# A fused two-block transformer kernel: all weight splits outside the top-k on VectorE, and every moving operand at one place within a KiB

## The chip, the core and the metric

The kernel runs on one core of one Trainium2 chip, as one launch. The metric is the device time of an execution in microseconds (us). The engines are named as in the profile: PE is TensorE's matmul, PEld its weight load, DVE is VectorE, ACT ScalarE, POOL GpSimd, SP SyncE, which issues most DMAs.

## What is computed

256 tokens of width 1024 go through a first block (windowed attention, a bidirectional RG-LRU, cross-attention to a memory, a gated merge, then a PEER layer of 16,384 experts) and through two hybrid layers (retention, a causal convolution of 31 taps, spatial gating, sliding-window attention, a gated merge, a gated FFN). All of it is float32. Cut to what matters here:

```python
h = rmsnorm(x, g_mix); proj = h @ w_in; ...          # first block
x = x + merged @ w_out
x = x + peer_ffn(rmsnorm(x, g_ffn), w_peer_q, sub_keys, u_tab, v_tab)
for l in range(2):                                    # hybrid layers
    z = rms_norm(x, norm1_g[l]) @ w_in[l]
    u = lax.conv_general_dilated(a * sigmoid(gate), conv_w, ...)   # 31 taps, per channel
    mix = jnp.sum(gates * branches, axis=2)
    x = x + mix @ w_out[l]
    gt, up = jnp.split(rms_norm(x, norm2_g[l]) @ w_ffn_in[l], 2, axis=-1)
    x = x + (silu(gt) * up) @ w_ffn_out[l]
```

The PEER layer is computed densely: `peer_u` and `peer_v` are multiplied whole, and the gates, which a top-k chooses, are spread over all experts by one-hot products.

## The kernel before

**Weights.** All weight matrices are cut into 128x128 blocks, and the host packs the 5416 blocks in the order of use. `Stream` (L41) brings them in: `_slot` (L69) takes eight blocks, a slot, and there are 677 slots. For a slot, SP loads the float32 values (`raw`, two slots in one 1 MB DMA, two buffers), ACT copies them rounded to float32r (`whi`, L88), and a subtraction leaves the rest (`wlo = raw - whi`, L91). This subtraction runs on DVE or on POOL: `pool_share = (m, d)` gives POOL the slots with `n * m % d < m`. In the program before it is (1, 2), every second slot, through the first block; (1, 1), every slot, from the second projection of the top-k; (0, 1), none, while the experts are computed; and (1, 2) again for both hybrid layers. `whi` and `wlo` have three buffers each, so the split runs up to three slots ahead of PE.

**Matmuls.** A product of two float32 matrices is three matmuls in float32r (`mm3`, L169): high by high, low by high, high by low. The weight block is the stationary operand, an activation row of 128 x 256 the moving one. One slot is 24 such matmuls.

**Activations.** `hh` and `hl` (L379, L380) hold the normed input's high and low part for every projection; `ga` holds the experts' activations. Other moving operands come from tiles of each stage's pool: `T8`, `T6`, `T4` of the first block (L415 to L422), `T4` of a layer (L1065), `fh`, `fl` and `raw` of the FFN. In the built program, `hh`, `hl` and `ga` start 704 bytes behind a multiple of 1024 bytes in a partition; the `T4` tiles of the layers at 352; the first block's tiles at ten places between 192 and 864; `fh` and `fl` at 192; the last three experts' `tail` at 64.

**Order.** The program is written as coroutines (`add`, `tick`): every second block taken from the stream gives waiting tasks a step, so convolution, attention and top-k are interleaved with the projections. A scheduling layer then sets the order on each engine, and each engine works through its list in that order. The slots' work has a high priority. The convolution of a layer is 124 instructions on DVE (L1121, "taps"), two for each step of its task and each issued after the latest subtraction on DVE (`tc.issue_after(ws.on_vector)`, L1120). DVE also does the low half of each activation split (L185, L188), the softmax sums and most evacuations; POOL adds up the gated merge (L621), a few products (L558, L1269, L1363) and some splits of a norm (L185).

Of the kernel before, what the change touches and what calls it, by code (L numbers as in the profile page):

```python
# [7 lines left out]
F32 = mybir.dt.float32  # L8
# [11 lines left out]
P = 128  # L20
S = 256
KD = 8
# [2 lines left out]
PRIO = 3000  # L25
RAW_BUFS = 2
SLOT_BUFS = 3
N_HA = 96
HALF = 64
TK_PACE = 20  # L30
# [22 lines left out]
class Stream:  # L53
# [3 lines left out]
    def __init__(self, K, pool, w):  # L57
        self.K, self.pool, self.w = K, pool, w
        self.order = []
        self.ticked = 0  # L60
        self.raw = None
        self.cur = None
        self.pool_share = (1, 2)

    def _dram(self, i):
        return self.w[i].rearrange("p (b c) -> p b c", c=P)
# [7 lines left out]
    def _slot(self):  # L74
        K, nc = self.K, self.K.nc
        n = len(self.order) // 8
        with K.tc.high_priority(offset=PRIO):
# [7 lines left out]
            src = self.raw[:, (n % 2) * 8:(n % 2) * 8 + 8, :]  # L85
            hi = self.pool.tile([P, 8, P], F32R, tag="whi", name="whi", bufs=SLOT_BUFS)
            lo = self.pool.tile([P, 8, P], F32R, tag="wlo", name="wlo", bufs=SLOT_BUFS)
            self.on_scalar = nc.scalar.activation(out=hi, in_=src, func=AF.Copy).ins  # L88
# [39 lines left out]
class Core:  # L128
# [111 lines left out]
    def transpose(self, out, in_):  # L240
        self.nc.tensor.transpose(out, in_, self.ident)

    def scr(self, name):
        return self.tp.tile([P, S], F32, tag="scr", name=name, bufs=N_SCR)

# [164 lines left out]
    def block1(self):  # L410
        tc, nc, a, ws = self.tc, self.nc, self.a, self.ws
        with ExitStack() as st:
            p = st.enter_context(tc.tile_pool(name="b1", bufs=1))

            def T8(dt=F32R):  # L415
                return p.tile([P, KD, S], dt, tag="t8", name="t8", bufs=2)

            def T6(dt=F32, w=S):
                return p.tile([P, 6, w], dt, tag="t6", name="t6", bufs=8)

            def T4(dt=F32):
                return p.tile([P, 4, S], dt, tag="t4", name="t4", bufs=5)  # L422

            def raw16():
                b = blocks(T6(F32R), T6(F32R), T6(F32R))
# [13 lines left out]
            t_rel = self.add(self.rel_bias(p), REL_AT)  # L439


            xl = T6(w=S + 3)
            nc.gpsimd.memset(xl[:, :, 0:2], 0.0)
            nc.gpsimd.memset(xl[:, :, S + 2:S + 3], 0.0)

# [288 lines left out]
    def peer(self):  # L734
# [4 lines left out]
        tc, nc, a, ws = self.tc, self.nc, self.a, self.ws  # L739
        with ExitStack() as st:  # L740
            p = st.enter_context(tc.tile_pool(name="pe", bufs=1))
# [5 lines left out]
            ga = [p.tile([P, 2, S], F32R, tag=f"ga{i}", name="ga") for i in range(2)]  # L747
            ha = p.tile([P, N_HA, S], F32, tag="ha", name="ha")
            hb = None

            def h(b):
                return ha[:, b, :] if b < N_HA else hb[:, b - N_HA, :]

# [17 lines left out]
            with tc.tile_pool(name="peg", bufs=1) as gp:  # L771
                hb = gp.tile([P, NBLK - N_HA, S], F32, tag="hb", name="hb")
                ws.pool_share = (0, 1)
# [5 lines left out]
                def build(c0, done):  # L779
# [19 lines left out]
                    def products(i, e2, m):  # L799
                        for o in range(0, T_OH, 4):  # L800
                            pg = self.bg.tile([P, 4, 2, HALF], F32, tag="bg", name="pgb")
                            for t in range(4):
# [9 lines left out]
                                                    op=ALU.add)  # L812
                            for b, t, c1, c2 in ((ha, 0, 0, N_HA), (hb, N_HA, N_HA, NBLK)):
                                k0, k1 = max(c1, c0), min(c2, c0 + w)
# [25 lines left out]

                cut = NBLK - N_HA
                for b0 in range(early, HALF, 4):
                    for b, k0, k1 in ((ha, b0, min(b0 + 4, HALF, cut)), (hb, max(b0, cut), min(b0 + 4, HALF))):
                        if k0 < k1:
                            o = HALF if b is ha else HALF - N_HA
                            nc.vector.tensor_tensor(out=ha[:, k0:k1, :], in0=ha[:, k0:k1, :],
# [29 lines left out]
                        u_block(ahead, h(ahead - done))  # L876
                        ahead += 1
                assert ahead == NBLK
                ws.pool_share = (1, 2)
                tl = self.tp.tile([P, LAST, 2, S], F32R, tag="ld", name="tail", bufs=1)  # L880
                tail = [weighted(NBLK - LAST + i, tl[:, i]) for i in range(LAST)]
            with tc.tile_pool(name="per", bufs=1) as gp:
# [40 lines left out]
    def topk(self, tp, i1, i2, gt, iot):  # L923
        nc, a, ws = self.nc, self.a, self.ws
# [85 lines left out]
        qts = {0: self.ld}  # L1010

        def picks():
            with self.tc.issue_after(ws.on_pool):
                nc.gpsimd.tensor_copy(io, self.cst[:, None, C_IO:C_IO + 16].to_broadcast([P, 32, 16]))
            for hq in range(4):
                for t in range(2):
                    while hq not in qts:
                        yield 1
                    unit(hq, t, qts[hq])
                    if hq == t == 1:  # L1020
                        with self.tc.issue_after(ws.on_pool):
                            nc.gpsimd.tensor_copy(iot, self.cst[:, C_IO:C_IO + P, None].to_broadcast([P, P, 2]))
                    yield TK_PACE
                    if hq == 3:
                        gates(t)
                        yield 2
                        turn(t)
            yield 4
# [25 lines left out]
    def mixers(self, l):  # L1054
        tc, nc, a, ws = self.tc, self.nc, self.a, self.ws
        with ExitStack() as st:
            p = st.enter_context(tc.tile_pool(name=f"m{l}", bufs=1))
            par = p.tile([P, P2_COLS], F32, tag="par2", name="par2")
            nc.scalar.dma_start(out=par, in_=a["par2"][l])
# [3 lines left out]
                return par[:, o:o + n]  # L1063

            def T4(dt=F32):  # L1065
                return p.tile([P, 4, S], dt, tag="t4", name="t4", bufs=13)

            def tmp(shape, tag, bufs=2, dt=F32):
                return p.tile(shape, dt, tag=tag, name=tag, bufs=bufs)
# [365 lines left out]
    def ffn(self, l):  # L1435
        tc, nc, a, ws = self.tc, self.nc, self.a, self.ws
        with ExitStack() as st:
            p = st.enter_context(tc.tile_pool(name=f"f{l}", bufs=1))
            fh = p.tile([P, FF, S], F32R, tag="fh", name="fh")
            fl = p.tile([P, FF, S], F32R, tag="fl", name="fl")  # L1440

# [167 lines left out]
```

## Time and profile before

| | |
|---|---|
| median of 3 runs | 2208.46 us (2206.96 to 2214.88) |
| the profiled execution | 2205.13 us |
| its span, first to last instruction | 2203.3 us |
| granted clock of PE, mean | 0.971 |
| PE busy | 2067.6 us (94%), 16818 matmuls |
| DVE busy | 1741.0 us (79%) |
| ACT busy | 1159.6 us (53%) |
| POOL busy | 734.2 us (33%) |

Stages in the profiled execution, by the first use of their slots: the first block to 350 us, the top-k to 500, the experts to 1189, layer 0's mixers to 1537 and its FFN to 1700, layer 1's mixers to 2042 and its FFN to the end. In each layer the first 155 to 165 us of the mixers hold the attentions, the retention and over half of the convolution; after them come the gated merge and the output projection. A busy PE is not a PE at its peak: every matmul is shown with about 280 ns, and matmuls that overlap follow each other at 113 ns or more, so a gap of less than some 170 ns does not show as idle time.

### The profile page before, as it was taken

To read this page: it belongs to the slowest core of one execution; us is meant where nothing else is said; L and a number is where in the kernel's file an instruction comes from. 1 tells how busy PE (TensorE), PEld (TensorE's weight loads), DVE (VectorE), ACT (ScalarE), POOL (GpSimd) and SP (SyncE) were. 2 spreads that over 40 slices of the span, in tenths; PEclk is the share of its full clock that TensorE was granted. 3 is DMA by queue.
4 is the path that set the end of the run, shared out by engine and by line. 5 is a ranking of instruction groups with operands and counts; after the bars stand their busy time and mean duration, and the time that the engine had idled before them with its cause. 6 is when DMAs were issued, how large, how long until landed. Compare 5 with 4: busy or idle time off the path is not lost. (4 is left out here: it accounts for less than half of the span.)

```text
span 2203.3 us, 41676 instructions
## 1 busy us (share of the span) xinstructions
PE 2067.6 (94%) x16818; PEld 2002.5 (91%) x16818; DVE 1741.0 (79%) x3117; ACT 1159.6 (53%) x1906; POOL 734.2 (33%) x361
## 2 busy tenths in 40 slices
PE   8879999959998999999998899999999889999999
PEld 7868999959998999999998778999999778999997
DVE  8837668998999888975557999976764999976772
ACT  5648654435554555545445555466555545465543
POOL 4424746830000000000003434654444434654443
PEclk9989999979999999999999999999999999999999
DMA  5343555424553444455554533454555533445554
GB/s 194 122 126 118 189 183 181 172 84 167 179 181 138 173 173 173 173 177 194 197 188 145 190 125 143 173 183 176 197 192 193 191 131 135 168 177 175 192 192 159
DMA packets 56925, 370.03 MB, mean 168 GB/s; under 512 B 6491, under 2 KB 10140, under 8 KB 13468
## 3 DMA queue, kind: packets, MB, share of 16 engines
q1 hardware_dynamic: 50256, 357.06, 45.5%
q10 hardware_dynamic: 6476, 10.31, 1.8%
q8 instruction: 131, 2.15, 0.4%
q14 instruction: 62, 0.51, 0.1%
HBM read 364.73 MB, written 2.62 MB: 167 GB/s over the span
## 5 line engine op out<-in xcount | busy, mean ns | idle before, releaser
L88 ACT ACTIVATE whi<-raw 128x1024 fp32r<-128x1024 f32 x677 | 716.5, 1060 | 731.0 <-PE acc L172 165.9
L91 POOL TENSOR_TENSOR wlo<-raw,whi 128x1024 fp32r<-128x1024 f32 x247 | 617.5, 2501 | 1324.6 <-ACT whi L88 1238.6
L91 DVE TENSOR_TENSOR wlo<-raw,whi 128x1024 fp32r<-128x1024 f32 x430 | 545.2, 1268 | 211.7 <-ACT whi L88 209.9
L171 PE MATMUL pu<-hh,whi 128*128 128x256 f32 x1024 | 291.0, 284 | 21.9 <-ACT whi L88 21.9
L173 PE MATMUL mm<-hh,wlo 128*128 128x256 f32 x1008 | 285.7, 284 | 7.3 <-DVE wlo L91 5.0
L173 PE MATMUL pu<-hh,wlo 128*128 128x256 f32 x1024 | 286.5, 280 | 0.0
L172 PE MATMUL pu<-hl,whi 128*128 128x256 f32 x1024 | 286.4, 280 | 0.0
L172 PE MATMUL mm<-hl,whi 128*128 128x256 f32 x1008 | 285.2, 283 | 0.0
L171 PE MATMUL mm<-hh,whi 128*128 128x256 f32 x1008 | 284.7, 282 | 0.0
L172 PE MATMUL acc<-ga,whi 128*128 128x256 f32 x1000 | 269.8, 279 | 5.1 <-DVE ga L185 5.1
L173 PE MATMUL acc<-ga,wlo 128*128 128x256 f32 x1000 | 269.2, 279 | 0.0
L171 PE MATMUL acc<-ga,whi 128*128 128x256 f32 x1000 | 249.3, 281 | 4.9 <-ACT ga L184 4.9
L1121 DVE SCALAR_TENSOR_TENSOR t<-up,hw,t 128x256 f32<-128x256 f32 x240 | 215.3, 901 | 3.7
L171 PEld LDWEIGHTS pu<-hh,whi 128*128 128x128 f32 x1024 | 195.3, 191 | 22.3 <-ACT whi L88 22.3
L173 PE MATMUL pg<-hh,wlo 128*128 128x256 f32 x704 | 198.9, 283 | 9.4 <-POOL wlo L91 6.3
L173 PEld LDWEIGHTS mm<-hh,wlo 128*128 128x128 f32 x1008 | 193.1, 192 | 11.2 <-DVE wlo L91 6.2
L171 PE MATMUL pg<-hh,whi 128*128 128x256 f32 x704 | 198.5, 282 | 1.2 <-ACT whi L88 1.2
L172 PE MATMUL pg<-hl,whi 128*128 128x256 f32 x704 | 197.4, 280 | 0.0
L172 PEld LDWEIGHTS mm<-hl,whi 128*128 128x128 f32 x1008 | 193.5, 192 | 2.9 <-issue 2.7
L171 PEld LDWEIGHTS mm<-hh,whi 128*128 128x128 f32 x1008 | 193.1, 192 | 1.5 <-issue 0.8
L172 PEld LDWEIGHTS pu<-hl,whi 128*128 128x128 f32 x1024 | 194.4, 190 | 0.0
L173 PEld LDWEIGHTS pu<-hh,wlo 128*128 128x128 f32 x1024 | 194.3, 190 | 0.0
(410 smaller groups left out, 5209.5 us busy)
## 6 DMA issues: line engine op xcount, KB each, us to landing
raw<-in_w SPq DMA_DIRECT2D x336, 1024.0 KB, 4.8
raw<-in_w SPq DMA_DIRECT2D x5, 512.0 KB, 5.5
bias<-bias_scr ACTq DMA_DIRECT2D x4, 512.0 KB, 6.8
bias_scr<-sbb ACTq DMA_DIRECT2D x4, 384.0 KB
cl<-in_cstl ACTq DMA_DIRECT2D x2, 576.0 KB, 3.7
x<-in_xT SPq DMA_DIRECT2D x4, 256.0 KB, 6.5
memt<-in_memT ACTq DMA_DIRECT2D x1, 1024.0 KB, 4.9
keys<-in_keysT ACTq DMA_DIRECT2D x1, 1024.0 KB
```

The lines of the kernel that those rows point to most:

```text
L88: self.on_scalar = nc.scalar.activation(out=hi, in_=src, func=AF.Copy).ins
L91: i = eng.tensor_tensor(out=lo, in0=src, in1=hi.bitcast(F32), op=ALU.subtract)
L171: mm(out, lhsT=wh, rhs=xh, start=start, stop=False)
L172: mm(out, lhsT=wh, rhs=xl, start=False, stop=False)
L173: mm(out, lhsT=wl, rhs=xh, start=False, stop=stop)
L1121: nc.vector.scalar_tensor_tensor(out=cy[:, j, :], in0=up[:, j, i:i + S], scalar=hw[:, j * NT + i:j * NT + i + 1], in1=cy[:, j, :], op0=ALU ...
```

## The change

It makes two edits at once.

- `pool_share` starts as (0, 1), and the line that put it back to (1, 2) after the experts is gone. So POOL subtracts only in the top-k, and DVE everywhere else. The copy of `io` for the top-k, on POOL, is issued after the latest subtraction on DVE, since there is no earlier one on POOL.
- The pools of the first block, of both layers' mixers and of both FFNs begin with a tile `pad` of 512 bytes per partition, which DVE fills with zeros and nobody reads. The tiles that matmuls read as moving operand (`T8`, `T6`, `T4`) go to a pool of their own (`pa`) right behind it; `xl`, whose rows are three elements longer, leaves `T6`. In the built program all these tiles, `fh`, `fl` and `raw` included, start 704 bytes behind a multiple of 1024, as `hh`, `hl` and `ga` do. `tail` stays at 64.

```diff
+PAD = 128
 class Stream:
-        self.pool_share = (1, 2)
+        self.pool_share = (0, 1)
 class Core:
+    def pad(self, pool):
+        self.nc.vector.memset(pool.tile([P, PAD], F32, tag="pad", name="pad"), 0.0)
     def block1(self):
+            pa = st.enter_context(tc.tile_pool(name="b1a", bufs=1))
+            self.pad(pa)
             p = st.enter_context(tc.tile_pool(name="b1", bufs=1))
             def T8(dt=F32R):
-                return p.tile([P, KD, S], dt, tag="t8", name="t8", bufs=2)
-            def T6(dt=F32, w=S):
-                return p.tile([P, 6, w], dt, tag="t6", name="t6", bufs=8)
+                return pa.tile([P, KD, S], dt, tag="t8", name="t8", bufs=2)
+            def T6(dt=F32):
+                return pa.tile([P, 6, S], dt, tag="t6", name="t6", bufs=8)
             def T4(dt=F32):
-                return p.tile([P, 4, S], dt, tag="t4", name="t4", bufs=5)
+                return pa.tile([P, 4, S], dt, tag="t4", name="t4", bufs=5)
-            xl = T6(w=S + 3)
+            xl = p.tile([P, 6, S + 3], F32, tag="xl", name="xl")
     def peer(self):
                 assert ahead == NBLK
-                ws.pool_share = (1, 2)
     def topk(self, tp, i1, i2, gt, iot):
         def picks():
-            with self.tc.issue_after(ws.on_pool):
+            with self.tc.issue_after(ws.on_vector):
                 nc.gpsimd.tensor_copy(io, ...)
     def mixers(self, l):
+            pa = st.enter_context(tc.tile_pool(name=f"a{l}", bufs=1))
+            self.pad(pa)
             p = st.enter_context(tc.tile_pool(name=f"m{l}", bufs=1))
             def T4(dt=F32):
-                return p.tile([P, 4, S], dt, tag="t4", name="t4", bufs=13)
+                return pa.tile([P, 4, S], dt, tag="t4", name="t4", bufs=13)
     def ffn(self, l):
             p = st.enter_context(tc.tile_pool(name=f"f{l}", bufs=1))
+            self.pad(p)
```

The built program shows how instructions move. First DVE in layer 0's mixers, while the first sliding-window attention (`sm`, `t_15109`) and the rotary embedding of the retention (`w_15197`, `t_14992`) run beside the taps (`t_14802<-up,hw`). Before:

```order
L91 TENSOR_TENSOR wlo<-raw,whi 128x1024
L1121 SCALAR_TENSOR_TENSOR t_14802<-up,hw,t_14802 128x256
L1226 TENSOR_SCALAR sm<-sm 128x4
L1264 TENSOR_TENSOR w_15197<-t_14992,cl 64x512 x2
L1121 SCALAR_TENSOR_TENSOR t_14802<-up,hw,t_14802 128x256
L1267 TENSOR_TENSOR t_14992<-t_14992,cl 128x512
L1121 SCALAR_TENSOR_TENSOR t_14802<-up,hw,t_14802 128x256
L1231 TENSOR_TENSOR sm<-sm 128x4
L1121 SCALAR_TENSOR_TENSOR t_14802<-up,hw,t_14802 128x256
L1232 RECIPROCAL sm<-sm 128x4
L1233 TENSOR_TENSOR t_15109<-t_15109,sm 128x4x128
L91 TENSOR_TENSOR wlo<-raw,whi 128x1024
```

The same place in the changed program, whose line numbers are 1 to 9 higher:

```order
L92 TENSOR_TENSOR wlo<-raw,whi 128x1024
L1234 TENSOR_TENSOR sm<-sk,sm 128x4
L1130 SCALAR_TENSOR_TENSOR t_14813<-up,hw,t_14813 128x256
L1235 TENSOR_SCALAR sm<-sm 128x4
L92 TENSOR_TENSOR wlo<-raw,whi 128x1024
L1130 SCALAR_TENSOR_TENSOR t_14813<-up,hw,t_14813 128x256 x3
L1240 TENSOR_TENSOR sm<-sm 128x4
L1130 SCALAR_TENSOR_TENSOR t_14813<-up,hw,t_14813 128x256
L1241 RECIPROCAL sm<-sm 128x4
L1130 SCALAR_TENSOR_TENSOR t_14813<-up,hw,t_14813 128x256
L1242 TENSOR_TENSOR t_15120<-t_15120,sm 128x4x128
L92 TENSOR_TENSOR wlo<-raw,whi 128x1024
```

Where DVE had one subtraction for two slots and four taps behind it, it now has one for each slot and mostly two taps behind it, with one to five in places. Over the whole program 208 subtractions come to DVE: 430 before, 638 now.

Second POOL, from the end of the experts to layer 0's gated merge. Before:

```order
L887 TENSOR_TENSOR gg<-par 128x8
L91 TENSOR_TENSOR wlo<-raw,whi 128x1024 x5
L185 TENSOR_TENSOR hl<-nh,hh 128x256 x3
L1100 MEMSET up 128x4x30
L91 TENSOR_TENSOR wlo<-raw,whi 128x1024 x5
L1349 TENSOR_TENSOR wst<-wst,cl 128x512
L91 TENSOR_TENSOR wlo<-raw,whi 128x1024
L1269 TENSOR_TENSOR t_14992<-t_14992,w_15104 128x512
L91 TENSOR_TENSOR wlo<-raw,whi 128x1024
L1269 TENSOR_TENSOR t_14992<-t_14992,w_15197 128x512
```

Now:

```order
L894 TENSOR_TENSOR gg<-par 128x8
L186 TENSOR_TENSOR hl<-nh,hh 128x256 x3
L1109 MEMSET up 128x4x30
L1358 TENSOR_TENSOR wst<-wst,cl 128x512
L1278 TENSOR_TENSOR t_15003<-t_15003,w_15115 128x512
L1278 TENSOR_TENSOR t_15003<-t_15003,w_15208 128x512
```

POOL keeps its own work in the same order, and 39 of its 247 subtractions, all in the top-k.

## Rows read from the trace of the kernel before

**Rows 1.** The page's first part: busy time, share of the span and instructions of PE, PEld, DVE, ACT and POOL.

```profile
PE 2067.6 (94%) x16818; PEld 2002.5 (91%) x16818; DVE 1741.0 (79%) x3117; ACT 1159.6 (53%) x1906; POOL 734.2 (33%) x361
```

**Rows 2.** Busy time by stage (windows): start and end of the stretch in us, its length, then busy time and instructions of PE, PEld, DVE, ACT and POOL, the granted clock, the DMA share and GB/s. The first two are the first block, the third the experts; then layer 0's convolution stretch and its gated merge with the output projection; then the same two in layer 1.

```profile
0.00:192.00 192.00, 156.27 (x1080) 142.28 (x1081) 133.70 (x274) 116.38 (x214) 77.12 (x47) 0.89 0.45 143
192.00:350.00 158.00, 151.58 (x1247) 149.62 (x1247) 110.80 (x152) 100.58 (x162) 81.24 (x45) 0.99 0.50 174
500.00:1189.00 689.00, 676.26 (x6039) 672.18 (x6040) 555.46 (x1124) 355.66 (x611) 11.19 (x5) 0.99 0.49 175
1189.00:1354.00 165.00, 145.34 (x962) 131.25 (x961) 151.91 (x260) 86.85 (x156) 62.59 (x30) 0.92 0.43 151
1354.00:1537.00 183.00, 175.88 (x1479) 173.89 (x1479) 152.07 (x195) 97.44 (x154) 101.51 (x52) 1.00 0.48 173
1700.00:1855.00 155.00, 139.87 (x957) 125.42 (x956) 140.66 (x235) 85.47 (x151) 59.62 (x29) 0.96 0.45 156
1855.00:2042.00 187.00, 180.12 (x1496) 177.72 (x1496) 157.30 (x200) 99.92 (x159) 103.09 (x54) 0.99 0.48 170
```

**Rows 3.** DVE's instructions by form in layer 0's convolution stretch, 1189 to 1354 us: line, engine, operation, tiles, shapes and count, then busy us and mean ns of one, then the idle time before them.

```profile
L1121 DVE SCALAR_TENSOR_TENSOR t<-up,hw,t 128x256 f32<-128x256 f32 x69 | 53.4, 777 | 1.0
L91 DVE TENSOR_TENSOR wlo<-raw,whi 128x1024 fp32r<-128x1024 f32 x20 | 27.4, 1370 | 2.0 <-ACT whi L88 2.0
L919 DVE SCALAR_TENSOR_TENSOR x<-x,par,rb 128x256 f32<-128x256 f32 x8 | 7.5, 1008 | 0.0
L257 DVE TENSOR_TENSOR nacc<-nacc,nsq 128x256 f32<-128x256 f32 x6 | 4.5, 774 | 0.1
L185 DVE TENSOR_TENSOR hl<-nh,hh 128x256 fp32r<-128x256 f32 x5 | 3.7, 735 | 0.2 <-ACT hh L184 0.2
```

**Rows 4.** All taps of both layers: shortest, median and longest in ns, first and last start.

```profile
L1121 DVE SCALAR_TENSOR_TENSOR t<-up,hw,t x240: 424/485/2733, 1224.2 to 1932.8; 128x256 f32<-128x256 f32 x120
```

**Rows 5.** Instructions in order of time (start in us, duration in us): DVE and POOL around 1241 us, in the convolution stretch, and around 1609 us, in layer 0's FFN.

```profile
1240.32 0.48 DVE L1121 SCALAR_TENSOR_TENSOR t<-up,hw,t 128x256 f32<-128x256 f32 x1
1240.86 2.38 POOL L91 TENSOR_TENSOR wlo<-raw,whi 128x1024 fp32r<-128x1024 f32 x1 [5.54 <-DVE t L1121]
1241.03 2.49 DVE L1121 SCALAR_TENSOR_TENSOR t<-up,hw,t 128x256 f32<-128x256 f32 x1
...
1608.98 2.40 POOL L91 TENSOR_TENSOR wlo<-raw,whi 128x1024 fp32r<-128x1024 f32 x1 [3.04 <-ACT whi L88]
1609.24 2.42 DVE L185 TENSOR_TENSOR fl<-fsg,fh 128x256 fp32r<-128x256 f32 x1 [1.46 <-ACT fh L184]
```

**Rows 6.** DVE's instructions by form where POOL is idle (the first: 500 to 1180 us) or seldom beside them (the second: 1537 to 1700 us); columns as in rows 3.

```profile
L91 DVE TENSOR_TENSOR wlo<-raw,whi 128x1024 fp32r<-128x1024 f32 x224 | 273.5, 1222 | 99.8 <-ACT whi L88 99.7
...
L257 DVE TENSOR_TENSOR nacc<-nacc,nsq 128x256 f32<-128x256 f32 x7 | 2.9, 412 | 0.0
```

**Rows 7.** The window 600 to 690 us of the experts; columns as in rows 2.

```profile
600.00:690.00 90.00, 90.00 (x843) 89.46 (x842) 83.50 (x181) 48.22 (x90) 0.00 (x0) 1.00 0.49 177
```

**Rows 8.** The two largest forms of DVE in layer 1's convolution stretch, 1700 to 1855 us; columns as in rows 3.

```profile
L1121 DVE SCALAR_TENSOR_TENSOR t<-up,hw,t 128x256 f32<-128x256 f32 x68 | 52.9, 782 | 1.0
L91 DVE TENSOR_TENSOR wlo<-raw,whi 128x1024 fp32r<-128x1024 f32 x19 | 26.9, 1414 | 2.2 <-ACT whi L88 2.1
```

**Rows 9.** What PE waited for, us in total, times, longest: in 1189 to 1354 us.

```profile
PE ptt L241 <- DVE t L1233: 8.2, 2, 4.8
PE pn L270 <- DVE nacc L257: 4.4, 1, 4.4
PE mm L179 <- DVE wlo L91: 3.2, 1, 3.2
PE pq L241 <- DVE w L1187: 3.0, 1, 3.0
```

**Rows 10.** The same in 1340 to 1540 us (the first two) and in 0 to 192 us (the last four).

```profile
PE pg L173 <- POOL wlo L91: 2.3, 3, 0.9
PE pp L173 <- DVE wlo L91: 2.1, 1, 2.1
...
PE mm L177 <- ACT whi L88: 12.9, 1, 12.9
PE po L662 <- ACT pts L658: 6.9, 2, 5.7
PE pb L285 <- DVE nrs L277: 2.7, 2, 2.1
PE mm L173 <- DVE wlo L91: 2.0, 2, 1.2
```

**Rows 11.** Windows of PE alone (stretch, length, PE busy and matmuls, clock, DMA share, GB/s): the FFN of layer 0, with operands at 704 and 192, and the output projection of layer 0, with `T4` operands at 352.

```profile
1560.00:1680.00 120.00, 120.00 (x1061) 1.00 0.54 194
1490.00:1530.00 40.00, 40.00 (x338) 1.00 0.52 185
```

**Rows 12.** The window 820 to 940 us of the experts, where all 256-column operands are `hh`, `hl` and `ga`, at 704: the matmuls into `acc` (PE and PEld), those into `pu` (PE, PEld and ACT), and the 128-column one-hot products into `pgb` (PE).

```profile
820.00:940.00 120.00, 79.11 (x633) 76.14 (x634) 0.00 (x0) 1.00 0.50 176
820.00:940.00 120.00, 39.87 (x315) 37.92 (x314) 5.13 (x14) 1.00 0.50 176
820.00:940.00 120.00, 10.23 (x128) 1.00 0.50 176
```

**Rows 13.** What ACT waited for longest in 440 to 475 us, at the end of the top-k.

```profile
ACT ge L988 <- DVE ge L987: 24.3, 1, 24.3
```

## The prediction

> **What bounds the kernel now.** I read the page's first part, then the busy time by stage, then what PE waits for, then DVE's forms and single instructions in order of time. PE is shown busy 94% of the span, DVE 79%, POOL 33% [rows 1]. A mean says little here: the experts and the FFNs are PE's, and nearly nothing is lost there (676.3 of 689 us in the experts, although DVE is busy for 555 of them) [rows 2]. The loss sits where POOL subtracts and DVE is crowded. In layer 0's convolution stretch PE is idle for 165 - 145.3 = 19.7 us, and the granted clock falls to 0.92, which is some 0.08 x 165 = 13.2 us of work: up to 33 us. DVE is busy for 151.9 of these 165 us. In layer 1's the two are 15.1 and 0.04 x 155 = 6.2 us, together 21, with DVE at 140.7 of 155. The gated merges lose 7.1 and 6.9 us, the first block's two parts 35.7 and 6.4 us [rows 2]. In layer 0's stretch the longest waits all end at DVE: softmax, norm sums, a subtraction, the q norm [rows 9].
>
> The reader should then see why DVE is crowded. Taps have a median of 485 ns and a longest of 2733 [rows 4], and the stretch's mean is 777 [rows 3]. One tap at 1240.32 takes 0.48 us; the one at 1241.03, behind the start of a POOL subtraction of 2.38 us, takes 2.49. In the FFN a split of 128x256 takes 2.42 us beside POOL's 2.40 [rows 5], where the same form elsewhere takes 412 ns (L257) [rows 6]. So a DVE instruction with two operands in SBUF that begins while POOL subtracts does not get on until POOL is done.
>
> **The change, part by part.**
>
> *The subtractions.* 208 of POOL's 247 go to DVE, at 1222 ns each where POOL is idle [rows 6]: 254 us more on DVE, and some 500 us less on POOL. DVE gets back what it lost to POOL. In layer 0's stretch: 69 taps x (777 - 485) = 20.1 us; 20 subtractions x (1370 - 1222) = 3.0; L919, of the taps' form, 8 x (1008 - 485) = 4.2; L257 6 x (774 - 412) = 2.2; `hl` 5 x (735 - 412) = 1.6: 31.1 us, smaller forms left out [rows 3, 4, 6]. It gets POOL's 20 subtractions, which are as many as its own since every second slot is POOL's: 24.4 us. DVE then has 151.9 - 31.1 + 24.4 = 145 us of work. How crowded may DVE be before PE waits? In the experts it is busy for 83.5 of 90 us, 92.8%, and PE for all 90 [rows 7]. By that share the stretch is 145.2 / 0.928 = 156.5 us, 8.5 less; by PE alone it is 165 - 33 = 132. I take 146, 19 us less, nearer the middle than DVE's end because the smaller forms come on top and because a tap that is not held up lets the softmax and norm steps behind it start sooner. In layer 1's stretch the taps give 68 x (782 - 485) = 20.2 us and the subtractions 19 x (1414 - 1222) = 3.6 [rows 8]; with 8 for the other forms as in layer 0, DVE has 140.7 - 31.8 + 24.4 = 133 us, and the ends are 143.7 and 133.7: I take 140, 15 us less.
>
> In the gated merges DVE and PE are not crowded for long; waits for POOL's and DVE's subtractions make up 4.4 of layer 0's 7.1 idle us [rows 10]. I take 4 us in each layer, 8 in all. In the first block's first part, 19.8 of the 35.7 idle us end at ACT, in two waits [rows 10], behind slow DMA issues that the change leaves in ACT's list. Of the other 16 I take 5, with 3 for the clock (0.89 there [rows 2]), and 3 of the 6.4 in the second part: 11.
>
> In the top-k POOL keeps every subtraction. Its end is set by DVE, ACT holding up the next slots behind one exp that waits 24.3 us for DVE [rows 13]; two or three slots before it move to DVE, about 3 us, and as many of POOL's holds go. Nothing. In the experts nothing changes. In the FFN the long splits get shorter, but PE never waits there (120.00 of 120 us [rows 11]): nothing.
>
> *The place of the moving operands.* In the FFN a 256-column matmul follows the one before after 120 / 1061 = 113.1 ns; in the output projection, with `T4` at 352, after 40 / 338 = 118.3 [rows 11]. The operands that change place and are not at 113 already (merge 1152 matmuls, output projections 576, the RG-LRU's gates 72, `mk` 96, the norm's raw leads 480) come to 2376, so all of them at 113.1 is 2376 x 5.2 = 12 us. But with every operand at 704, from 820 to 940 us, 948 matmuls took what the one-hot products left, (120 - 10.2) / 948 = 115.8 ns at the least [rows 12]: the right place allows the short spacing and does not secure it. Ends 0 and 12; I take 6.
>
> Here a rule speaks against this edit. The Trainium skill (TensorE: Matmul & The Clock Gate, "Back-to-back issue gap") gives a spacing by the number of columns alone, 262 cycles for 256, about 109 ns at 2.4 GHz, wherever the operand lies. By it this term is 0 and the sum 6 us higher; the two spacings of rows 11 differ at a granted clock of 1.00, which it does not explain.
>
> *The pads.* Five fills of 128x128, and no reader; DVE's nearest row is the 412 ns of a 128x256 subtraction [rows 6], so 2 us at the most on an engine with room, and nothing if they lie beside other work. I take 0.
>
> **Sum.** 19 + 15 + 8 + 11 + 6 = 59 us. The profiled execution took 2205.1 us, so 2146; that execution is 3.3 us below the median of the runs shown, which I neglect. What a measurement of this kernel can tell from no change is about 0.5%, 11 us: the three runs shown spread over 8.
>
> **The rivals.**
>
> *Place does not matter.* The two spacings come from what ran beside the matmuls, not from the address. For: the slow spacing with all operands at 704 [rows 12]. Against: DVE and POOL are busy in the FFN too. The term of 6 goes: 2152.
>
> *DVE takes it back.* Subtractions go into DVE's list behind up to five taps, and the crowd stays: the stretches end at 156.5 and 143.7 (20 us less in place of 34), and the softmax and q norm waits [rows 9] remain, so the merges and the first block give only half, 9. With 3 for the place that is 32: 2173. If even the 8.5 us fail, nothing but a few us is left: 2198, no change.
>
> *Slower.* The long taps are not POOL's doing, or POOL's remaining work holds them as long. Then DVE gets 24.4 us in each convolution stretch and gets nothing back: 151.9 + 24.4 = 176.3 us of work in 165, and 165.1 in 155. With PE waiting for it all, that is 11 + 10 us, and at the experts' 92.8% it is 190 and 178, 25 + 23 us. I take 40 with the first block: 2245. It decides where DVE gets back less than the 24.4 us it is given; the taps alone give back 20.1. Against it stands the row in which one tap of 0.48 becomes 2.49 us just under POOL's instruction [rows 5].
>
> *More.* Both stretches come down to PE's bound: 33 + 21 in place of 34, and the place gives its 12: 2120.
>
> **How the numbers follow.** Chances: the forecast 0.40; place does not matter 0.19; more 0.09; DVE takes it back 0.15; no change 0.09; slower 0.08. The forecast's own range is 2125 to 2165, from the ends of its terms. The range must keep 0.8: it reaches from 2112 to 2190, which leaves out no change, slower and a few hundredths of the rest. Faster by more than 0.5% means below 2194: 0.40 + 0.19 + 0.09 + 0.15 = 0.83. No change 0.09, slower 0.08.
>
> **What would show it.** In the profile after, POOL is busy for about 215 us (734.2 less 208 subtractions at some 2.5) and its `wlo` group has 39 instructions. DVE's has 638, at 1.22 to 1.25 us outside the top-k. The taps' mean falls from 777 to under 550 ns; if it stays above 700, the mechanism is wrong. DVE is busy for at least 85% of the convolution stretches, which last about 146 and 140 us, and PE's waits for `t`, `w` and `nacc` of DVE there are half of now. The granted clock's mean rises above 0.975. The output projections' matmuls come at 113 to 116 ns; if they stay at 118, the place is not what sets them. The FFNs and the experts last as long as now to within 3 us. A wait of PE on ACT's `whi` in the stretches where now it waits on DVE would mean that ACT's list has become the bound.

## The result, and the profile after

The changed kernel takes **2144.25 us** (median of 4 runs, 2133.95 to 2170.02), the kernel before 2210.15 beside it; the ratio is **0.967 [0.961, 0.973]**. The longest run, at a granted clock of 0.929, counts in the median but not in the ratio, which has a fifth run of 2131.19 us in its place and amounts to 72 us. The forecast was 2146 us within 2112 to 2190. The profiled execution took 2153.45 us, 9 more than the median, and had a span of 2151.7.

The stages are compared by the stream's slots: a stage lasts from PE's first matmul on the weights of its first slot to the first on the next stage's. Times in us, each of one profiled execution; the last three columns are experiments (below), the last but one the changed kernel once more.

| stage (slots) | before | change | share alone, again | change, again | three edits more |
|---|---|---|---|---|---|
| first block (0-89) | 341.4 | 329.1 | 330.1 | 326.1 | 311.1 |
| top-k (90-129) | 150.8 | 154.3 | 152.6 | 152.7 | 117.5 |
| experts (130-359) | 687.9 | 696.1 | 682.6 | 687.0 | 705.5 |
| convolution, layer 0 (360-399) | 165.0 | 151.2 | 149.7 | 149.3 | 141.5 |
| gated merge and output projection, layer 0 (400-459) | 183.4 | 170.2 | 174.9 | 170.1 | 170.1 |
| FFN, layer 0 (460-519) | 163.2 | 169.6 | 169.7 | 163.2 | 163.2 |
| convolution, layer 1 (520-559) | 154.7 | 139.2 | 141.4 | 140.7 | 136.6 |
| merge, layer 1 (560-619) | 186.6 | 172.5 | 176.1 | 172.5 | 172.6 |
| FFN, layer 1 (620-676) | 161.8 | 160.4 | 160.5 | 160.4 | 160.4 |

The first part of the page after, against [rows 1]: POOL falls from 734.2 to 227.1 us; DVE falls from 1741.0 to 1682.0, although it has 208 subtractions more.

```profile
PE 2051.8 (95%) x16818; PEld 1993.0 (93%) x16818; DVE 1682.0 (78%) x3330; ACT 1165.2 (54%) x1910; POOL 227.1 (11%) x153
```

The same windows as [rows 2], moved to where the stages now begin, with layer 0's FFN (the sixth line) added:

```profile
0.00:183.20 183.20, 151.50 (x1085) 139.11 (x1086) 126.70 (x295) 111.09 (x212) 30.17 (x24) 0.92 0.46 150
183.20:338.00 154.80, 151.84 (x1258) 150.45 (x1257) 111.23 (x176) 103.33 (x162) 23.44 (x23) 0.99 0.50 178
...
492.00:1188.50 696.50, 685.48 (x6035) 681.36 (x6036) 555.64 (x1132) 355.07 (x611) 0.21 (x1) 0.99 0.49 174
1188.50:1339.70 151.20, 139.80 (x958) 124.00 (x957) 134.22 (x266) 88.33 (x156) 11.64 (x9) 0.95 0.46 163
1339.70:1510.00 170.30, 170.30 (x1487) 170.16 (x1486) 146.90 (x237) 101.36 (x159) 27.94 (x23) 1.00 0.52 184
1510.00:1679.50 169.50, 169.50 (x1441) 169.50 (x1441) 96.77 (x126) 82.72 (x119) 0.00 (x0) 1.00 0.53 189
1679.50:1818.80 139.30, 133.12 (x951) 121.00 (x950) 127.07 (x249) 87.30 (x151) 12.20 (x9) 0.99 0.49 173
1818.80:1991.20 172.40, 172.17 (x1502) 171.78 (x1501) 145.72 (x236) 102.13 (x161) 25.66 (x23) 1.00 0.51 184
```

In the two convolution stretches DVE's work falls by 17.7 and 13.6 us, PE's idle time from 19.7 to 11.4 and from 15.1 to 6.2, and the clock rises from 0.92 and 0.96 to 0.95 and 0.99. In the merges PE has next to no idle time left (0.0 and 0.2 us).

DVE's largest forms in layer 0's convolution stretch (line, operation, tiles, count, busy us, mean ns), which answer to [rows 3], and all taps, which answer to [rows 4]:

```profile
L92 DVE TENSOR_TENSOR wlo<-raw,whi 128x1024 fp32r<-128x1024 f32 x40 | 48.8, 1219 | 7.6 <-ACT whi L89 7.4
L1130 DVE SCALAR_TENSOR_TENSOR t<-up,hw,t 128x256 f32<-128x256 f32 x70 | 34.6, 508 | 0.3
...
L926 DVE SCALAR_TENSOR_TENSOR x<-x,par,rb 128x256 f32<-128x256 f32 x8 | 3.3, 477 | 0.0
...
L186 DVE TENSOR_TENSOR hl<-nh,hh 128x256 fp32r<-128x256 f32 x5 | 2.0, 416 | 0.0
...
L262 DVE TENSOR_TENSOR nacc<-nacc,nsq 128x256 f32<-128x256 f32 x5 | 1.9, 422 | 0.0
```

```profile
L1130 DVE SCALAR_TENSOR_TENSOR t<-up,hw,t x240: 422/478/1525, 1217.1 to 1887.9; 128x256 f32<-128x256 f32 x120
```

The tap's median hardly changed (485 to 478 ns); its mean fell from 777 to 508 because the long ones went. Single instructions of DVE (start, us) at the place of [rows 5] show the tap now behind a subtraction of DVE's own and not held:

```profile
1238.85 0.48 DVE L1130 SCALAR_TENSOR_TENSOR t<-up,hw,t 128x256 f32<-128x256 f32 x1
1239.25 1.22 DVE L92 TENSOR_TENSOR wlo<-raw,whi 128x1024 fp32r<-128x1024 f32 x1
...
1240.99 0.48 DVE L1130 SCALAR_TENSOR_TENSOR t<-up,hw,t 128x256 f32<-128x256 f32 x1
```

What PE waits for in that stretch (total us, times, longest), against [rows 9]:

```profile
PE ptt L242 <- DVE t L1242: 7.0, 2, 4.0
PE mm L174 <- DVE wlo L92: 1.3, 2, 1.0
PE pb L290 <- DVE nrs L919: 1.3, 1, 1.3
PE mm L180 <- DVE wlo L92: 0.8, 2, 0.7
PE pn L275 <- DVE nacc L262: 0.4, 1, 0.4
```

The softmax, norm sums and q norm together went from 15.6 to 7.4 us; what is left is the softmax's (`ptt`).

### The profile page after: what moved, and what is told of

The parts are those of the page before. It is cut to its first block, busy times and chain, and to the rows that moved or that the text cites. A ratio compares the mean times of both kernels' runs of the same rounds, so it can differ in the third digit from the quotient of the medians.

```text
span 2151.7 us, 41502 instructions
## 1 busy us (share of the span) xinstructions
PE 2051.8 (95%) x16818; PEld 1993.0 (93%) x16818; DVE 1682.0 (78%) x3330; ACT 1165.2 (54%) x1910; POOL 227.1 (11%) x153
## 4 chain that ended last, share of the span: by engine, by line
PE 74%; DVE 16%; DMA 4%; ACT 3%; issue 2%; ACTq 0%; POOL 0%; SPq 0%; DVEq 0%
PE mm L174 6%; PE mm L172 6%; PE mm L173 6%; PE acc L173 5%; PE acc L174 5%; PE acc L172 5%; PE pu L172 4%; PE pu L173 4%; PE pu L174 4%; PE pg L174 3%; PE pg L172 3%; PE pg L173 3%; DVE wlo L92 3%; DMA raw<-in_w 2%; PE mml L172 2%
## 5 line engine op out<-in xcount | busy, mean ns | idle before, releaser
L92 DVE TENSOR_TENSOR wlo<-raw,whi 128x1024 fp32r<-128x1024 f32 x638 | 789.9, 1238 | 343.3 <-ACT whi L89 341.2
L173 PEld LDWEIGHTS acc<-ga,whi 128*128 128x128 f32 x1000 | 189.5, 189 | 4.2 <-DVE ga L186 4.2
L174 PEld LDWEIGHTS acc<-ga,wlo 128*128 128x128 f32 x1000 | 189.2, 189 | 0.0
```

Source lines behind the costliest of these rows:

```text
L92: i = eng.tensor_tensor(out=lo, in0=src, in1=hi.bitcast(F32), op=ALU.subtract)
L173: mm(out, lhsT=wh, rhs=xl, start=False, stop=False)
L174: mm(out, lhsT=wl, rhs=xh, start=False, stop=stop)
```

## The experiments

**Each part alone.** Share alone is the kernel before with

```diff
-        self.pool_share = (1, 2)
+        self.pool_share = (0, 1)
...
-                ws.pool_share = (1, 2)
...
-            with self.tc.issue_after(ws.on_pool):
+            with self.tc.issue_after(ws.on_vector):
```

> The kernel before with only the first part of the change: all subtractions outside the top-k on DVE; the moving operands stay where they were. If POOL's hold on DVE's two-operand instructions is what was lost, and the place gave its 6 us: about 2150 us (2138 to 2162), the taps' mean near 500 ns in both layers, the two convolution stretches near 151 and 139 us, the output projections' 256-column matmuls still at 118 ns or more. If the place gave all of its 12 us: 2156. If the place is what shortened the stretches: above 2190, with taps near 777 ns. If the place does nothing: the time of the changed kernel within 5 us, 2144.

Place alone is the changed kernel with these three edits the other way round.

> The kernel before with only the second part: the moving operands at 704 mod 1024, POOL keeping every second subtraction. If the place is worth 6 us: about 2204 us; 12 us: 2198; nothing: 2210. In each of these the taps' mean stays at 740 to 800 ns and the convolution stretches at 160 to 168 and 150 to 158 us; the output projections' matmuls come at 113 to 114 ns if the place sets their spacing, at 118 if it does not. If the two parts need one another (the place only pays off where PE does not wait), this run is at 2210 and the other at 2155 or more.

Measured: share alone 2146.06 us, ratio 0.970 [0.967, 0.972]; stretches 149.9 and 143.1 us, taps 514 and 506 ns. Place alone 2208.49, ratio 0.999 [0.996, 1.001]; stretches 163.4 and 152.7 us, taps 856 and 779 ns. So nearly all of the gain comes from moving the subtractions. By itself the place is worth 2.5 us, which this measurement cannot tell from nothing.

**What the place is worth beside the share**, on one chip:

> The changed kernel once more, beside the share alone on the same chip, to settle what the place of the operands is worth where all subtractions are on DVE. The first four times spread over 2134 to 2153 us. If the place is worth the 6 us of the forecast there: its ratio to the share alone is near 0.997, some 2137 to 2141 against 2143 to 2147. If it is worth its upper end, 12: near 2133. If nothing: within 2 us of each other. What decides which spacing a stretch falls into is not in the code, so the profiled execution may show 113 or 118 ns in layer 0's FFN and in the experts.

> The share alone once more, on the same chip as the changed kernel: 2143 to 2149 us as before. Its T4 operands lie at 352, 736, 672 and 768, so the gated merges with the output projections take 174 to 177 us each, against 169 to 173 with the operands at 704, whatever the experts and the FFN do in this execution.

Measured: 2138.30 us, 0.968 [0.965, 0.971], and 2147.15 us, 0.973 [0.968, 0.977]: 8.9 us apart, with intervals that overlap. The stage it was meant for is clearer. Layer 0's and 1's merge with output projection, first the changed kernel again, then the share alone again (columns as in [rows 2]):

```profile
1323.60:1493.80 170.20, 170.20 (x1487) 170.06 (x1487) 146.53 (x236) 101.24 (x158) 28.01 (x23) 1.00 0.52 183
1797.70:1970.20 172.50, 172.37 (x1503) 172.11 (x1501) 145.82 (x236) 102.24 (x161) 25.68 (x23) 1.00 0.52 184
```

```profile
1323.50:1498.50 175.00, 174.49 (x1487) 174.29 (x1485) 147.67 (x240) 102.73 (x161) 30.00 (x23) 1.00 0.51 179
1809.50:1985.70 176.20, 175.42 (x1503) 175.19 (x1501) 147.42 (x240) 104.35 (x163) 27.04 (x23) 1.00 0.51 180
```

PE has next to no idle time to lose in either (0.8 us at most); the same matmuls take 4.8 and 3.7 us less at the new place. The first pair of executions gave the same (170.2 and 172.5 against 174.7 and 176.1).

**Which place?** The pads got other sizes after the top-k, so that `T4`, `fh` and `fl` lie elsewhere (`(0, 40)[l]` and `(40, 64)[l]` in the first run, `(136, 16)[l]` and `(4, 32)[l]` in the second):

```diff
-            self.pad(pa)
+            self.pad(pa, (0, 40)[l])
...
-            self.pad(p)
+            self.pad(p, (40, 64)[l])
```

> The changed kernel with other places within a KiB after the top-k: T4 tiles at 192 in layer 0 and at 352 in layer 1, fh and fl at 352 in layer 0's FFN and at 448 in layer 1's. If one place alone (704) allows the short spacing: the merges' matmuls on T4 and both output projections at 117 to 121 ns, and the FFNs' last matmuls too. If 192 is as good as 704 (the FFN of the kernel before ran at 113 with fh and fl at 192): layer 0's output projection at 113 to 114, layer 1's at 118 or more, both FFN ends above 117. If the place does not matter: either of 113.3 and 117.8 ns in each, with no tie to the place. The time: 2144 to 2152.

> The changed kernel with four more places after the top-k: T4 at 736 in layer 0 and 256 in layer 1, fh and fl at 224 in layer 0's FFN and 320 in layer 1's. So far 256-column matmuls came at 113.3 or 117.8 ns with operands at 704, 192 and 448, and at 119 to 120 with operands at 352. If what matters is whether the place is a multiple of 64 bytes: layer 0's output projection and its FFN's last third at 119 to 121 ns (736 and 224 are not), layer 1's at 113.3 or 117.8 (256 and 320 are). If it takes a multiple of 64 that leaves 192 within 256: all four at 119 or more. If 352 was bad for being different from hh's place: all four at 119 or more too, and then 192 and 448 of the run before are left unexplained.

Measured: 2148.55 us, 0.972 [0.968, 0.975], and 2148.47 us in one run. Windows of PE inside output projections (length, matmuls); first the changed kernel, `T4` at 704:

```profile
1481.00:1505.00 24.00, 24.00 (x213) 1.00 0.50 176
```

First run, layer 0 at 192 and layer 1 at 352:

```profile
1460.00:1485.00 25.00, 25.00 (x222) 1.00 0.57 203
1940.00:1970.00 30.00, 30.00 (x254) 1.00 0.51 176
```

Second run, layer 0 at 736 and layer 1 at 256:

```profile
1465.00:1490.00 25.00, 25.00 (x214) 1.00 0.53 184
1940.00:1970.00 30.00, 30.00 (x253) 1.00 0.51 184
```

That is 112.7 ns at 704, 112.6 at 192, and 118.1, 116.8 and 118.6 at 352, 736 and 256. The first run shows it within one stage too: in layer 0's FFN, the matmuls on `hh` and `hl` (704) come at 113.0 ns (708 from 1500 to 1580 us), and those on `fh` and `fl` (352) behind them at 119.4 ns:

```profile
1600.00:1640.00 40.00, 40.00 (x335) 1.00 0.50 181
```

So it is not "the same place as `hh`" that counts (192 is not), and not a multiple of 64 bytes, as I had supposed for the second run (256 is one). 704 and 192 are alike, 512 bytes apart; five places settle no rule. In layer 1's FFN (448 and 320) `fh` turned out not to be a moving operand of 256 columns, so those two places say nothing; nor does 224 in layer 0's of the second run, where `hh` ran long too (117.4 ns, and `fh` 117.3).

**Is it POOL's hold?** (The hold: DVE's two-operand instructions wait while POOL works.) In the changed kernel, POOL gets useless work on every second slot of the hybrid layers' mixers (not of their FFNs), in layer 0 the subtraction, in layer 1 a copy:

```diff
+            if self.extra and n % 2 == 0:
+                kind, sx = self.extra
+                if kind == "sub":
+                    nc.gpsimd.tensor_tensor(out=sx, in0=src, in1=hi.bitcast(F32), op=ALU.subtract)
+                else:
+                    nc.gpsimd.tensor_copy(sx, src)
...
+            ws.extra = (("sub", "copy")[l], p.tile([P, 8, P], F32, tag="sx", name="sx"))
...
+            ws.extra = None
```

> The changed kernel, DVE doing all subtractions as there, with useless work on POOL for every second slot of the two hybrid layers (not in the FFNs): in layer 0 POOL does the same subtraction once more into a tile that nobody reads, in layer 1 it copies raw into that tile, the same size with one operand. Hold theory: in layer 0 a POOL subtraction holds DVE as before, the taps' mean is 700 ns or more, DVE's work in the convolution stretch goes from 134 to some 160 us and the stretch from 151 to 165 to 180 us. In layer 1, if what holds DVE is any POOL instruction on SBUF, taps near 780 ns and the stretch at 155 to 170 us; if only one with two operands, taps near 500 ns and the stretch near 139. Rival (the taps were long for another reason, such as where they stood in DVE's list): taps near 500 ns in both layers, stretches at 151 and 139 us, the time that of the changed kernel.

Measured: 2223.31 us, 1.005 [1.003, 1.007], 79 more than the changed kernel. The convolution stretches, layer 0's and layer 1's (columns as in [rows 2]):

```profile
1181.70:1357.80 176.10, 145.83 (x958) 127.48 (x957) 168.14 (x259) 86.50 (x153) 66.46 (x28) 0.94 0.40 138
...
1735.70:1885.00 149.30, 135.65 (x950) 121.92 (x949) 138.27 (x246) 85.96 (x149) 39.92 (x29) 0.98 0.47 162
```

Taps and POOL's useless work in layer 0, then in layer 1 (columns as in [rows 3]):

```profile
L1138 DVE SCALAR_TENSOR_TENSOR t<-up,hw,t 128x256 f32<-128x256 f32 x69 | 54.7, 803 | 0.2
...
L101 POOL TENSOR_TENSOR sx<-raw,whi 128x1024 f32<-128x1024 f32 x19 | 56.4, 2968 | 70.2 <-ACT whi L90 65.6 <-issue 4.1 <-PE mml L181 0.4
...
L1138 DVE SCALAR_TENSOR_TENSOR t<-up,hw,t 128x256 f32<-128x256 f32 x70 | 42.0, 608 | 0.5
...
L103 POOL COPY sx<-raw 128x1024 f32<-128x1024 f32 x20 | 29.1, 1454 | 95.8 <-DMA raw<-in_w 95.8
```

And one of each in order of time (start, us): a tap that begins under POOL's subtraction, and one that begins under POOL's copy.

```profile
1216.93 3.05 POOL L101 TENSOR_TENSOR sx<-raw,whi 128x1024 f32<-128x1024 f32 x1 [2.83 <-ACT whi L90]
1217.62 2.65 DVE L1138 SCALAR_TENSOR_TENSOR t<-up,hw,t 128x256 f32<-128x256 f32 x1
...
1773.83 1.06 POOL L103 COPY sx<-raw 128x1024 f32<-128x1024 f32 x1 [5.28 <-DMA raw<-in_w]
1774.21 0.95 DVE L1138 SCALAR_TENSOR_TENSOR t<-up,hw,t 128x256 f32<-128x256 f32 x1
```

DVE's list is the changed kernel's; only POOL is busy beside it. Taps are back at 803 ns and DVE's work grows from 134 to 168 us: the hold is shown. Neither of my two cases for layer 1 came true: a copy holds as well, but for its own, shorter time (1.06 us in the row above, 1.36 in the median of 47), so the taps stop at 608 ns and the stretch at 149.3. The Trainium skill (SBUF — State Buffer, "SBUF: two separate sides") says that a VectorE instruction with two SBUF inputs and a GpSimd instruction that reads SBUF take one port pair in turn, the later one waiting out the whole of the first. The trace agrees: 1217.62 + 2.65 lies 0.29 us behind POOL's end. Of the 79 us, 25 and 10 lie in the two convolution stretches and 38 and 9 in the merges (208.3 and 181.3 us); there the useless work also stands ahead of POOL's own merge sums and keeps the `raw` buffers longer (ACT waits 37.0 us for `raw` in layer 0's, 18.6 without it), so the merges do not show the hold alone.

**How many?** POOL gets every fourth subtraction outside the top-k and the experts:

```diff
-        self.pool_share = (0, 1)
+        self.pool_share = (1, 4)
...
+                ws.pool_share = (1, 4)
```

> The changed kernel with POOL doing every fourth subtraction outside the top-k, in place of none or every second one. Per subtraction, POOL spared DVE 1.22 us in the convolution stretch and cost it about 31.1 / 20 = 1.55 us in instructions held up. If the hold is the whole effect and it goes by the number of subtractions: DVE's work in layer 0's stretch is between 134 and 152 us (about 143 at half), the stretch near 158 us and the time near half way, 2165 to 2185. If DVE's own load mattered as much as the hold, a quarter would be better than none: below 2140, with the stretch under 149 us.

Measured: 2172.62 us, 0.985 [0.982, 0.988], in the middle between none and half, as the hold theory had it; but not where it had it. Layer 0's stretch takes 149.5 us (DVE 139.0 us busy, taps 645 ns), no longer than without POOL. Layer 1's is longer by 5 us (145.4), and most of the loss is in the merges, 181.9 and 184.3 us, nearly what they took before. Layer 0's stretch and merge, columns as in [rows 2]:

```profile
1183.30:1332.80 149.50, 137.71 (x956) 123.10 (x955) 138.96 (x253) 86.34 (x154) 36.47 (x20) 0.98 0.46 166
1332.80:1514.70 181.90, 174.08 (x1488) 171.30 (x1487) 155.81 (x227) 104.07 (x161) 67.59 (x39) 1.00 0.48 171
```

In that merge the hold is back on DVE's splits of the merged activations: 0.96 us each, against 1.11 in the kernel before and 0.42 in the changed one. A quarter is not better than none.

**The top-k too.** The 39 subtractions that POOL kept go to DVE, and a copy (`iot`) that POOL issued behind the last of them follows DVE's latest:

```diff
-                        with self.tc.issue_after(ws.on_pool):
+                        with self.tc.issue_after(ws.on_vector):
...
-            ws.pool_share = (1, 1)
+            ws.pool_share = (0, 1)
```

> The changed kernel with the top-k's 39 subtractions on DVE as well, so that POOL has none. DVE is busy for 151.4 of the 154 us there, with POOL's subtractions beside it. If the hold costs less there than the subtractions would (most of the top-k's instructions have one operand): DVE gets 39 x 1.23 = 48 us and gives back at most a few us, the stretch goes from 154 to 185 to 200 us and the time to 2175 to 2190. If the hold costs as much there as in the convolution (20 subtractions on POOL had cost DVE 31 us there, so 39 some 60): the stretch becomes 10 us shorter and the time about 2134.

Measured: 2108.00 us, 0.954 [0.950, 0.957]. The second of my two cases came true, and it was too small: the stage shortens by 37 us (154.3 to 117.5), not 10. The two largest two-operand forms of the top-k, in the changed kernel and then here (columns as in [rows 3]):

```profile
L982 DVE TENSOR_TENSOR oh<-ijf,io 128x512 f16<-128x512 f16 x16 | 22.6, 1414 | 0.0
L985 DVE TENSOR_TENSOR oh<-oh,tf 128x512 f16<-128x512 f16 x16 | 19.8, 1235 | 0.2
```

```profile
L982 DVE TENSOR_TENSOR oh<-ijf,io 128x512 f16<-128x512 f16 x14 | 9.5, 678 | 0.0
...
L985 DVE TENSOR_TENSOR oh<-oh,tf 128x512 f16<-128x512 f16 x14 | 5.8, 416 | 0.0
```

These two alone give back 16 x (736 + 819) = 25 us, all forms some 55, for the 48 that the subtractions cost. That leaves about 7 us. The rest, as far as the order shows it, came from ACT's list: the exp that waits for DVE [rows 13] now stands behind the `whi` of eleven more slots. Its wait, in the changed kernel and then here:

```profile
ACT ge L995 <- DVE ge L994: 29.4, 2, 28.3
```

```profile
ACT ge L995 <- DVE ge L994: 4.6, 1, 4.6
```

PE's wait of 24.0 us for a `whi` behind that exp is gone with it. How the two shares divide was not tried apart.

**The softmax's transposes two slots later:**

```diff
-                yield 3
+                yield 5
                 nkb = nk // P
```

> The changed kernel with PE's transposes of the softmax two slots later in its list (five slots behind the scores in place of three). In the changed kernel PE waits for the softmax in each convolution stretch (7.0 and 5.0 us) and its clock is at the lower of its two levels after it. If DVE's list is what makes the softmax late, and the rest of the stretch has room: both waits go, the stretches shrink by 7 to 12 and 5 to 9 us, 2125 to 2132 us in all. If the stretch is bounded by DVE's work as a whole (134 of 151 us): the wait moves to another instruction, the stretch shortens by less than 3 us and the time stays within 5 us of 2144.

Measured: 2128.57 us, 0.963 [0.960, 0.965]. PE's waits for the softmax are gone, the stretches take 145.3 and 136.6 us in place of 149.3 and 140.7 (5.9 and 2.6 under the first profile of the change). DVE's work is as before, so it was the place of the wait in PE's list that cost, not DVE's load as a whole. The stretches give some 8 us of the median's 16; the rest is not traced to the edit (layer 0's FFN took 163.2 us and the experts 687.9, as in the second execution of the change). Layer 0's stretch and layer 1's, columns as in [rows 2]:

```profile
1177.30:1322.50 145.20, 138.02 (x962) 122.86 (x961) 133.97 (x271) 88.72 (x157) 10.86 (x10) 0.99 0.46 164
1655.10:1791.60 136.50, 132.87 (x954) 119.88 (x953) 127.49 (x254) 86.42 (x152) 10.78 (x10) 1.00 0.49 172
```

**The bias table earlier:**

```diff
-REL_AT = 20
+REL_AT = 8
```

> The changed kernel with the first block's table of position biases begun 12 slots earlier, so that the four DMA issues of ACT that took 0.3 and 8.2 us near 130 us stand elsewhere. If PE's longest wait of the first block (11.6 us, behind ACT) is theirs: the first part goes from 174 to 163 to 167 us, the time to 2134 to 2138. If they only move the wait, or another instruction of ACT holds PE there: no change, within 4 us of 2144.

Measured: 2117.68 us, 0.956 [0.953, 0.959]; the first block's first part takes 157.7 us in place of 174.2, more than PE's one wait. The whole first block is 17 us shorter (312.2) than in the first execution of the change, 14 than in the second; the median fell by 27, and the rest is not traced to the edit. The row of ACT in the changed kernel that explains it:

```profile
164.19 0.47 ACT L549 ACTIVATE lth<-mm,hbr 128x256 f32<-128x256 f32 x1 [13.54 <-DMA bias_scr<-sbb]
```

ACT does not wait for the issues alone but for the DMAs' end: `sbb`, their source, and `lth` share the three buffers of one tag (`b2`), so a tanh of the RG-LRU waits until the table is written. PE stands still for 11.57 us behind it and starts again at the lower clock (granted 0.50 from 160 to 165 us, 0.62 in the next five).

**All three on top of the change:**

> The changed kernel with three of the edits tried so far: the top-k's subtractions on DVE too, the softmax's transposes two slots later, the bias table 12 slots earlier. Alone they gave 36, 16 and 27 us against 2144. They lie in different stages (top-k, convolution stretches, first block), so if they add up: 2066 us (2060 to 2074). If one makes room that another had already made, or what they gave was in part a luckier spacing of matmuls elsewhere (113.3 in place of 117.8 ns): 2075 to 2095, with the three stretches as short as in the runs of one edit each.

Measured: **2088.18 us, 0.948 [0.945, 0.952]**, faster than both kernels, but some 20 us short of the sum (2066). The stretches keep what they had gained (last column of the table). Of the shortfall 10 us lie in the experts, 705.5 us against 695.8 with the top-k's edit alone. Two executions of one kernel differ there by nearly as much (696.1 and 687.0 us for the change). In 740 to 900 us PE has 1433 matmuls here (first line) and 1483 there (second), without idle time in either:

```profile
740.00:900.00 160.00, 160.00 (x1433) 1.00 0.49 173
```

```profile
740.00:900.00 160.00, 160.00 (x1483) 1.00 0.51 179
```

The rest is open. Part of it lies in the 2144 that the sum starts from: beside the second execution of the change (a span of 2130.6 us) the three edits save 29, 6 and 14 us, 50 together, and all three 43. Layer 0's convolution stretch, shorter in two of the three runs (148.7, 145.3, 143.9 against 149.3), is 141.5 here.

## Why the prediction was right, term by term

*The subtractions and the hold.* Right, and shown by putting the hold back. Of the signs named: POOL 227 us (215 said) with 39 `wlo`; DVE's 638 at 1.24 us; taps under 550 ns; DVE busy for 89 and 91% of the stretches; PE's waits named there 7.4 us of 15.6; the clock's mean 0.971 to 0.976. The wait on ACT's `whi` that would have shown ACT as the bound stayed at 0.2 and 0.3 us.

*Convolution stretches, 19 and 15 us.* 13.8 and 15.5 in the profiled execution, 15.3 and 13.3 with the share alone. One term was mis-sized: DVE got back more than the 31.1 us counted, its work came out at 134.2 and 127.1 us and not 145 and 133. By the experts' 92.8% layer 0's stretch would then be 144.6 us; it took 151.2, so DVE's load as a whole was not its bound. The softmax's steps, each behind taps and subtractions in DVE's list, still made PE wait 7.0 us, with the lower clock behind it (0.50 from 1300 to 1304 us); without that wait the stretch takes 145.3 us (above). That the stretch ended within 5 us of the 146 is in part luck.

*Gated merges, 4 us each.* The step that failed in size: 8.5 and 10.5 us with the share alone, 13.2 and 14.1 with both. I counted only the waits that end at a subtraction, 4.4 of 7.1 idle us [rows 10]; in fact all of the idle time went (7.1 and 6.9 us to 0.5 and 0.8 with the share alone), since the activations' splits and the merge's sums on DVE were held as well (1.11 and 0.86 us each in layer 0's merge before, 0.42 both with the share alone). The rest is time in which PE was shown busy, 1.4 and 4.7 us; it was not traced further.

*First block, 11 us.* 12.3 and 15.3. That the waits on ACT would stay was right; that slow issues were their cause was half of it, since ACT waits for the end of those DMAs too (above).

*Place, 6 us with ends 0 and 12.* 8.5 us in the merges beside the share, 2.5 alone. "Allows the short spacing and does not secure it" holds: 112.7 ns in the output projection, while layer 0's FFN and the experts (at 704 but for `tail`) ran long in this execution. The spacing by the number of columns alone that the Trainium skill gives (TensorE: Matmul & The Clock Gate, "Back-to-back issue gap") would have made this term 0; its 262 cycles for 256 columns stand there for a single matmul, not for a stream of weight loads and matmuls. No row shown here of 256-column matmuls alone has such a spacing: the shortest is 112.6 ns.

*Top-k, experts, FFN: nothing.* The top-k is 1.9 to 3.5 us longer. "As long as now to within 3 us" failed in the profiled execution, by 8.2 us in the experts and 6.4 in layer 0's FFN, and held in the next one (687.0 and 163.2). In the FFN it is the spacing, and not the change: the share alone, with the old places, has the long FFN too. (In its first execution that FFN took 163.3 us.) The changed kernel first, its FFN at 117.5 ns a matmul, then the share alone again, at 117.4 (before, 113.1 [rows 11]):

```profile
1560.00:1680.00 120.00, 120.00 (x1021) 1.00 0.52 185
```

```profile
1530.00:1650.00 120.00, 120.00 (x1022) 1.00 0.53 187
```

*The sum.* 59 us were said, 51.6 came in the profiled spans and 72.7 in the second execution; the median's 66 lies between. That it came out so close is luck: in the profiled spans the merges gave 27.3 us where 14 were said for them and the place, while the top-k, the experts and layer 0's FFN, where nothing was said, lost 18.1, and the stretches gave 29.3 in place of 34.

*The rivals.* "Place does not matter" is refuted by the output projections, though the place is worth little. "DVE takes it back" is refuted by the merges: their idle time went whole, not half; but the softmax wait that it named did stay (7.0 us of 8.2). "More" failed in the stretches, which came nowhere near PE's bound (151.2 and 139.2 us against 132 and 134). "Slower" had the right mechanism for a POOL that keeps its work: 176.3 us were priced for layer 0's stretch, and with the hold put back it took 176.1. The agreement is partly chance, for DVE was busy for only 168.1 of them.

## What to carry to other kernels

Two elementwise engines are not two where they hold each other up: count, for each instruction given to POOL, what DVE loses under it (here 1.8 us, 33.9 us for the 19 useless subtractions, where each real one would spare it 1.22), and look at the longest duration of a DVE form beside its median. Then look at what is left: three small edits gave some 50 us more (2138.3 to 2088.2), in part because a wait is paid by all that stands behind it in an engine's list. Two executions of one kernel can differ by a spacing of matmuls that no line of code sets, so compare stages, not totals, where a few us matter.

## What the runs showed of the hardware that was not expected

Matmuls of 256 columns come at either of two spacings at a granted clock of 1.00, 113 or 117.5 to 118 ns, in FFNs for a whole stage, in one execution this and in the next that (layer 0's FFN with its operands at 704 or 192: 163.2 to 163.8 or 169.6 to 169.7 us). With the moving operand at 352, 736 or 256 within a KiB the output projections were never at the short one (116.8 to 119.0 ns).

POOL's one-operand copy of 128x1024 (1.04 us at the least) holds a two-operand DVE instruction until its end, as its subtraction of that size does (2.4 us and more).
